# Gates of one branch moved from the merge stage into the RWKV stage's fillers, in a hybrid encoder layer on one Trainium2 core

## Chip, core and metric

The kernel runs on one core of one Trainium2 chip. The metric is the device time of one execution in microseconds (us). Lower is better.

## The reference

One encoder layer on 256 tokens of width 2048, all float32. Cut to what matters here:

```python
h = rms_norm(x, norm_mix_g)
a_cols, b_cols, c_cols, gate_cols = split(h @ w_in)
y_a = spatial_gating(a_cols)          # branch a
y_b = hyena_mixer(b_cols)             # branch b
y_c = rwkv7_mixer(c_cols)             # branch c: WKV scan, 16 heads, two directions
gates = sigmoid(gate_cols).reshape(bsz, seq, 3, D_MODEL)
merged = (gates[:, :, 0] * (y_a @ w_branch_a)
        + gates[:, :, 1] * (y_b @ w_branch_b)
        + gates[:, :, 2] * (y_c @ w_branch_c))
x = x + merged @ w_out
x = x + (silu(h2 @ w_ffn_gate) * (h2 @ w_ffn_up)) @ w_ffn_down     # h2 = rms_norm(x)
return rms_norm(x, norm_final_g)
```

A gate depends on `h` alone, which is known from the start. `y_c @ w_branch_c` needs all of `y_c`, so it can only be done when RWKV is over.

## The kernel before

**Dense products.** Activations stand channel by token: a tile has 128 channels by 256 tokens. Each float32 operand is split into a rounded high part and the rest, so that one product of a 128x128 weight block with 128x256 activations needs three matmuls: high by high, high by low, low by high. This kernel calls that a **step** of `dense` (L243 to L245, three matmuls of 256 columns). `dense_wide` does the same with two matmuls (L263: one of 512 columns that holds both parts of the activation, and L264: one of 256), and leaves two halves in PSUM that must be added afterwards. Weights come in **pieces** of four blocks, 256 KB: one DMA on SP's queue (L225), one cast on ACT (`wh`, L226), one subtraction (`wl`, L230) on DVE or POOL, whose share of the pieces is `pool_share`. There are five buffers each for `w`, `wh` and `wl`.

**RWKV and its fillers.** `rwkv` works on 8 pairs of heads. Each pair goes through five threads (preparation, scores, inverse, chain of four chunks, norm) made of small matmuls with DVE, ACT and POOL work between them. `threads` goes round all live threads, one part of each per **turn**. In each turn it also issues `ROUND` steps of dense work from a queue. That queue holds the projections of the next head pairs (`front`, labels c0 to c7, 48 steps each) and the merges of branch b (`merge_part`, label m, 16 steps for the gate and 8 for the branch, for each of 16 output tiles `n`). `more` feeds the queue. Where a projection isn't finished when its head pair starts, `need` issues the rest at once, with no thread's work between. What is left in the queue when the threads are done goes out in `drain`. Turns are a matter of program order; each engine runs its own instructions in that order and waits on semaphores.

**Last merges.** `merge_last` then does branch c for each `n`: 16 steps of `dense_wide` for the gate, two additions' worth of work and a tanh, 8 steps of `dense_wide` for the branch, and the sum into `macc`, whose split `mw` is the input of `outproj`. The sigmoid is written as tanh, with its factor folded in. In both versions the last part of an output is a chain through three engines: DVE (L1336) to POOL (L1337) to ACT (L1338) to DVE (L1339).

After that come `outproj` and `ffn`, which the change leaves alone.

The functions that the change touches, and their callers:

Of the kernel before, what the change touches and what calls it, by code (L numbers as in the profile page):

```python
# [9 lines left out]
F32 = mybir.dt.float32  # L10
F32R = mybir.dt.float32r
I32 = mybir.dt.int32
AF = mybir.ActivationFunctionType
ALU = mybir.AluOpType
PSUM = bass.MemoryType.PSUM

P = 128
T = 256
D = 2048
KD = D // P  # L20
# [10 lines left out]
KPIECE = 4  # L31
AHEAD = 3
LEN = {"conv": 9, "filter_mlp": 6, "filter_block": 14}
ROUND = 4.0
GC = 256
RS_MAGIC = float(0x5F1FFFF9)
RS_A = 2.38924456
# [87 lines left out]
def halves(x):  # L125
    return x[:, :, 0, :], x[:, :, 1, :]
# [68 lines left out]
class Build:  # L195
# [192 lines left out]
    def rwkv(self, rp, ych, ycl, y):  # L388
        nc, tc = self.nc, self.tc
        t = self.t  # L390
# [14 lines left out]
        for i in range(3):  # L405
            ps = self.pst("dn")
# [29 lines left out]

        front_weights = lambda j: [t["wc"][3 + 3 * j + i] for i in (1, 2, 0)]
        res, sts = {}, {}
        merges = iter(range(KD))

        def more():

            for n in merges:
                self.feed("m", self.merge_part(rp, n, 1, y, self.macc[:, n, :], False), (t["wgt"][n, 1], t["wbr"][n, 1]))
                return

        def preps():
            for j in range(NJ):
                self.need(f"c{j}")
                yield from self.wkv_prep(R, j, fronts[j], res)  # L450
                if j + 2 < NJ:
                    yield from self.after("v", j - 1)
                    self.feed(f"c{j + 2}", front(j + 2), front_weights(j + 2))

        def scores():
            for j in range(NJ):
                yield from self.after("prep", j)
                yield from self.after("chain", j - 2)
                yield from self.wkv_scores(R, j, res[j], sts)

        def inverses():
            for j in range(NJ):
                yield from self.after("blocks", j)
                yield from self.wkv_inverse(R, j, sts[j])

        def chains():
            for j in range(NJ):
                yield from self.after("inverse", j)
                yield from self.wkv_chain(R, j, res[j], sts.pop(j))

        def norms():
            for j in range(NJ):
                yield from self.after("chain", j)
                yield from self.wkv_norm(R, j, res.pop(j), ych, ycl)
# [3 lines left out]
        self.need("c0")  # L478
        self.pool_share = 0.6
        self.threads([norms(), chains(), inverses(), scores(), preps()], more)  # L480
        while len(self.queue) < KD:
            k = len(self.queue)
            more()
            if len(self.queue) == k:
                break
        self.drain()

    def threads(self, live, more):

        active, credit, still = 1, 0.0, 0  # L490
        while live:
            steps = 0
            for g in list(live):
# [3 lines left out]
                elif step:  # L497
                    steps += 1
                    credit += ROUND / active
                    while credit >= 1:  # L500
# [805 lines left out]
    def merge_part(self, p, n, b, y, out, first):  # L1306
# [10 lines left out]
        else:  # L1317
            nc.vector.scalar_tensor_tensor(th, th, 1.0, ps[:, :T], ALU.add, ALU.mult)
            nc.gpsimd.tensor_tensor(out, out, th, ALU.add)

    def merge_last(self, mp, y, mw):
        nc = self.nc
        for n in range(KD):
            m = self.macc[:, n, :]
            ps = self.pst("dn")
            self.dense_wide(self.t["wgt"][n, 2], lambda k: self.hw[:, k, :, :], ps)
            th = mp.tile([P, T], F32, tag="th", name="th", bufs=2)
            nc.vector.tensor_copy(th, ps[:, T:])
            nc.vector.tensor_tensor(th, th, ps[:, :T], ALU.add)
            nc.scalar.activation(th, th, AF.Tanh, scale=0.5)  # L1330
            ps = self.pst("dn")
            self.dense_wide(self.t["wbr"][n, 2], lambda k: y["c"][:, k, :, :], ps)
            s = mp.tile([P, T], F32, tag="s", name="s", bufs=2)
            nc.scalar.copy(s, ps[:, T:])
            nc.vector.tensor_tensor(s, s, ps[:, :T], ALU.add)
            nc.vector.scalar_tensor_tensor(th, th, 1.0, s, ALU.add, ALU.mult)  # L1336
            nc.gpsimd.tensor_tensor(m, m, th, ALU.add)  # L1337
            nc.scalar.activation(mw[:, n, 0, :], m, AF.Copy, scale=0.5)  # L1338
            nc.vector.scalar_tensor_tensor(mw[:, n, 1, :], m, 0.5, mw[:, n, 0, :].bitcast(F32), ALU.mult, ALU.subtract)  # L1339
# [102 lines left out]
```

## Time and profile before

| | us |
|---|---|
| median of three runs | 2011.07 (2007.12 to 2012.86) |
| the profiled execution, device time | 2020.24 |
| its span, first to last instruction | 2018.2 |
| busy PE, DVE, ACT, POOL | 1920.9, 1397.8, 1017.0, 562.2 |
| RWKV's turns, first to last of its small matmuls | 518.7 (510.4 to 1029.1) |
| dense work left over after them | 10.1 (1029.1 to 1039.2) |
| `merge_last` | 135.7 (1039.2 to 1174.9) |

Times of stages are those of PE's instructions. PE is TensorE (PEld its weight loads, which overlap), DVE is VectorE, ACT ScalarE, POOL GpSimd, SP the engine whose queue starts the weight DMAs. PEclk is the clock that TensorE was granted, 1.00 being 2.4 GHz and 0.50 being 1.2 GHz. "Busy" is a share of time with an instruction under way and not a measure of speed.

### The profile page before, as it was taken

To read this page: it belongs to the slowest core of one execution; us is meant where nothing else is said; L and a number is where in the kernel's file an instruction comes from. 1 tells how busy PE (TensorE), PEld (TensorE's weight loads), DVE (VectorE), ACT (ScalarE), POOL (GpSimd) and SP (SyncE) were. 2 spreads that over 40 slices of the span, in tenths; PEclk is the share of its full clock that TensorE was granted. 3 is DMA by queue.
4 is the path that set the end of the run, shared out by engine and by line. 5 is a ranking of instruction groups with operands and counts; after the bars stand their busy time and mean duration, and the time that the engine had idled before them with its cause. 6 is when DMAs were issued, how large, how long until landed. Compare 5 with 4: busy or idle time off the path is not lost.

```text
span 2018.2 us, 39307 instructions
## 1 busy us (share of the span) xinstructions
PE 1920.9 (95%) x14468; PEld 1734.5 (86%) x14468; DVE 1397.8 (69%) x2588; ACT 1017.0 (50%) x1958; POOL 562.2 (28%) x587
## 2 busy tenths in 40 slices
PE   7999999999879888998899999999999999999997
PEld 5899999999868787888898888888888888888886
DVE  7977788774777767677657667766666666655555
ACT  5665555545433344343445555555555555545443
POOL 5323232235645554455431121111111111100001
PEclk8999999999889899898999999999999999999999
DMA  7454444436343332333345565555555555666664
GB/s 233 159 167 156 142 146 144 155 132 197 115 105 95 103 99 84 105 104 91 104 151 186 187 225 188 187 190 190 190 191 190 189 190 191 190 187 185 187 187 136
DMA packets 215784, 320.51 MB, mean 159 GB/s; under 512 B 62182, under 2 KB 65768, under 8 KB 215592
## 3 DMA queue, kind: packets, MB, share of 16 engines
q1 hardware_dynamic: 209264, 306.13, 48.0%
q0 software_dynamic: 1984, 6.21, 1.0%
q10 hardware_dynamic: 4344, 5.67, 0.9%
q8 instruction: 113, 1.85, 0.4%
q14 instruction: 79, 0.65, 0.1%
HBM read 314.00 MB, written 3.93 MB: 158 GB/s over the span
## 4 chain that ended last, share of the span: by engine, by line
PE 82%; DVE 11%; DMA 3%; issue 2%; ACT 1%; SPq 0%; POOL 0%; DVEq 0%; ACTq 0%; POOLq 0%
PE ps_dn L263 23%; PE ps_dn L264 12%; PE ps_dn L243 9%; PE ps_big L263 8%; PE ps_dn L244 8%; PE ps_dn L245 8%; PE ps_big L264 4%; DVE Y L710 2%; PE ps_big L650 1%; DVE wl L230 1%; DVE Yt L709 1%; DMA Z<-d 1%; PE ps_ch L819 1%; PE ps_big L981 0%; DMA N<-d 0%
## 5 line engine op out<-in xcount | busy, mean ns | idle before, releaser
L226 ACT CAST wh<-w 128x512 fp32r<-128x512 f32 x1148 | 705.1, 619 | 655.0 <-PE ps_dn L263 260.6
L230 DVE TENSOR_TENSOR wl<-w,wh 128x512 fp32r<-128x512 f32 x945 | 711.4, 758 | 381.6 <-ACT wh L226 377.8
L243 PE MATMUL ps_dn<-hw,wh 128*128 128x256 f32 x1328 | 402.5, 303 | 1.6 <-ACT th L1312 1.2
L245 PE MATMUL ps_dn<-hw,wl 128*128 128x256 f32 x1328 | 382.9, 288 | 1.9 <-DVE wl L230 1.9
L244 PE MATMUL ps_dn<-hw,wh 128*128 128x256 f32 x1328 | 381.9, 288 | 0.0
L230 POOL TENSOR_TENSOR wl<-w,wh 128x512 fp32r<-128x512 f32 x203 | 273.3, 1350 | 383.9 <-ACT wh L226 345.0
L243 PEld LDWEIGHTS ps_dn<-hw,wh 128*128 128x128 f32 x1328 | 259.5, 195 | 12.4 <-issue 4.0
L245 PEld LDWEIGHTS ps_dn<-hw,wl 128*128 128x128 f32 x1328 | 259.5, 195 | 3.2 <-DVE wl L230 2.1
L244 PEld LDWEIGHTS ps_dn<-hw,wh 128*128 128x128 f32 x1328 | 259.7, 196 | 1.4
L263 PE MATMUL ps_dn<-gw,wh 128*128 128x512 f32 x704 | 246.3, 391 | 0.0
L263 PE MATMUL ps_big<-gw,wh 128*128 128x512 f32 x704 | 246.0, 391 | 0.0
L263 PE MATMUL ps_dn<-hid,wh 128*128 128x512 f32 x660 | 233.2, 396 | 0.0
L264 PE MATMUL ps_dn<-hid,wl 128*128 128x256 f32 x704 | 198.4, 282 | 0.0
L264 PE MATMUL ps_dn<-gw,wl 128*128 128x256 f32 x704 | 197.3, 280 | 0.0
L264 PE MATMUL ps_big<-gw,wl 128*128 128x256 f32 x704 | 197.1, 280 | 0.0
L263 PEld LDWEIGHTS ps_dn<-gw,wh 128*128 128x128 f32 x704 | 131.7, 187 | 28.9
L263 PEld LDWEIGHTS ps_big<-gw,wh 128*128 128x128 f32 x704 | 131.6, 187 | 28.9
L263 PEld LDWEIGHTS ps_dn<-hid,wh 128*128 128x128 f32 x660 | 124.0, 188 | 30.1
L264 PEld LDWEIGHTS ps_dn<-gw,wl 128*128 128x128 f32 x704 | 133.1, 189 | 0.1
L264 PEld LDWEIGHTS ps_big<-gw,wl 128*128 128x128 f32 x704 | 133.1, 189 | 0.0
L264 PEld LDWEIGHTS ps_dn<-hid,wl 128*128 128x128 f32 x704 | 132.2, 188 | 0.0
L1371 POOL TENSOR_TENSOR acc<-acc,sq 128x256 f32<-128x256 f32 x28 | 20.9, 745 | 292.3 <-ACT sq L1369 284.4
(395 smaller groups left out, 3369.0 us busy)
## 6 DMA issues: line engine op xcount, KB each, us to landing
w<-in_wgu_dram SPq DMA_DIRECT2D x352, 256.0 KB, 3.3
w<-in_wgt_dram SPq DMA_DIRECT2D x192, 256.0 KB, 3.1
w<-in_wdn_dram SPq DMA_DIRECT2D x176, 256.0 KB, 2.8
w<-in_wc_dram SPq DMA_DIRECT2D x108, 256.0 KB, 3.2
w<-in_wb_dram SPq DMA_DIRECT2D x96, 256.0 KB, 3.2
w<-in_wbr_dram SPq DMA_DIRECT2D x96, 256.0 KB, 2.7
w<-in_wo_dram SPq DMA_DIRECT2D x64, 256.0 KB, 3.4
w<-in_wav_dram SPq DMA_DIRECT2D x32, 256.0 KB, 3.7
```

The lines of the kernel that those rows point to most:

```text
L226: nc.scalar.copy(wh[:, :m], w[:, :m])
L230: e.tensor_tensor(wl[:, :m], w[:, :m], wh[:, :m].bitcast(F32), ALU.subtract)
L243: mm(ps, wh[:, i, :], xh[:, k, :], start=(k == 0), stop=False)
L244: mm(ps, wh[:, i, :], xl[:, k, :], start=False, stop=False)
L245: mm(ps, wl[:, i, :], xh[:, k, :], start=False, stop=(k == nk - 1))
L263: mm(ps, wh[:, i, :], xk.rearrange("p a t -> p (a t)"), start=(k == 0), stop=False)
L264: mm(ps[:, :T], wl[:, i, :], xk[:, 0, :], start=False, stop=(k == nk - 1))
L650: nc.tensor.matmul(ph[h][:, c * P:(c + 1) * P], bk[rows, d, c // 2, (c % 2) * P:(c % 2) * P + P], ar[rows, d, c, 1 - c % 2::1 + c % 2, :], ...
L709: V.tensor_tensor(z, N[:, k, k + 1:].unsqueeze(1).broadcast_to([P, w, n]), Y[:, :w, k:k + 1].broadcast_to([P, w, n]), mult)
L710: V.tensor_tensor(Y[:, :w, k + 1:], Y[:, :w, k + 1:], z, add)
L819: nc.tensor.matmul(pv[:, :P], ar[:, d, c, 0:2, :], R["sb"][i - 1][:, d, :], start=False, stop=(d == 1))
L1371: self.nc.gpsimd.tensor_tensor(acc, acc, s, ALU.add)
```

## The change

A new generator, `gate`, computes the gate of branch c for one output tile with 16 steps of `dense`, takes the tanh and stores the 128 KB result in a DRAM tensor, `gates`, by a DMA from POOL's queue. `more` now feeds merges of b and gates of c in turn, so the fillers of RWKV go from 768 steps to 1024. `ROUND` goes up by the same ratio, from 4 to 16/3. `merge_last` loads a gate by a DMA from POOL's queue, and does the branch with 8 steps of `dense` in place of 24 of `dense_wide`; the additions of PSUM halves and the tanh are gone from it.

```diff
-ROUND = 4.0
+ROUND = 16 / 3
...
-        merges = iter(range(KD))
+        self.gates = self.dp.tile([KD, P, T], F32, name="gates")
+        merges = iter([(n, b) for n in range(KD) for b in (1, 2)])
...
-            for n in merges:
-                self.feed("m", self.merge_part(rp, n, 1, y, self.macc[:, n, :], False), (t["wgt"][n, 1], t["wbr"][n, 1]))
+            for n, b in merges:
+                if b == 1:
+                    self.feed("m", self.merge_part(rp, n, 1, y, self.macc[:, n, :], False), (t["wgt"][n, 1], t["wbr"][n, 1]))
+                else:
+                    self.feed("g", self.gate(rp, n), (t["wgt"][n, 2],))
...
+    def gate(self, p, n):
+
+        ps = self.pst("dn")
+        yield from self.dense(self.t["wgt"][n, 2], self.hh, self.hl, ps[:, :T])
+        th = p.tile([P, T], F32, tag="th", name="th", bufs=1)
+        self.nc.scalar.activation(th, ps[:, :T], AF.Tanh, scale=0.5)
+        self.nc.gpsimd.dma_start(self.gates[n], th)
+
     def merge_last(self, mp, y, mw):
...
+            th = mp.tile([P, T], F32, tag="th", name="th", bufs=3)
+            nc.gpsimd.dma_start(th, self.gates[n])
             ps = self.pst("dn")
-            self.dense_wide(self.t["wgt"][n, 2], lambda k: self.hw[:, k, :, :], ps)
-            th = mp.tile([P, T], F32, tag="th", name="th", bufs=2)
-            nc.vector.tensor_copy(th, ps[:, T:])
-            nc.vector.tensor_tensor(th, th, ps[:, :T], ALU.add)
-            nc.scalar.activation(th, th, AF.Tanh, scale=0.5)
-            ps = self.pst("dn")
-            self.dense_wide(self.t["wbr"][n, 2], lambda k: y["c"][:, k, :, :], ps)
-            s = mp.tile([P, T], F32, tag="s", name="s", bufs=2)
-            nc.scalar.copy(s, ps[:, T:])
-            nc.vector.tensor_tensor(s, s, ps[:, :T], ALU.add)
-            nc.vector.scalar_tensor_tensor(th, th, 1.0, s, ALU.add, ALU.mult)
+            self.dense_all(self.t["wbr"][n, 2], *halves(y["c"]), ps[:, :T])
+            nc.vector.scalar_tensor_tensor(th, th, 1.0, ps[:, :T], ALU.add, ALU.mult)
```

Steps of `dense` in the order of PE's instructions, counted in the two built programs (the 1576 rows of small matmuls are the same in both):

| | before | after |
|---|---|---|
| between the first and the last small matmul of RWKV | 692 | 829 |
| of these issued at once by `need` | 77 | 9 |
| after the last small matmul, ahead of `merge_last` | 27 | 146 |
| in `merge_last` | 384 (wide) | 128 |

Lines from L440 on stand 4 or 5 lower in the changed kernel. On SP's queue, the last weight DMAs of RWKV before (`in_wgt_dram` holds gate weights, `in_wbr_dram` branch weights; the rows with d, N, Y and Z are RWKV's own):

```order
L225 DMA w<-in_wgt_dram 128x512 x3
L225 DMA w<-in_wbr_dram 128x512 x2
L225 DMA w<-in_wgt_dram 128x512
L716 DMA d_6479<-Y 32x8x16 x4
L225 DMA w<-in_wgt_dram 128x512 x2
L722 DMA Z<-d_6479 128x8x32
L225 DMA w<-in_wgt_dram 128x512
L225 DMA w<-in_wbr_dram 128x512 x2
L225 DMA w<-in_wgt_dram 128x512 x4
L225 DMA w<-in_wbr_dram 128x512 x2
L225 DMA w<-in_wgt_dram 128x512 x4
```

The same place after the change, down to the DMAs of `merge_last` (x32) and `outproj`:

```order
L225 DMA w<-in_wgt_dram 128x512 x6
L720 DMA d_6479<-Y 32x8x16 x4
L225 DMA w<-in_wbr_dram 128x512 x2
L726 DMA Z<-d_6479 128x8x32
L225 DMA w<-in_wgt_dram 128x512 x8
L225 DMA w<-in_wbr_dram 128x512 x2
L225 DMA w<-in_wgt_dram 128x512 x8
L225 DMA w<-in_wbr_dram 128x512 x2
...
L225 DMA w<-in_wgt_dram 128x512 x4
L225 DMA w<-in_wbr_dram 128x512 x32
L225 DMA w<-in_wo_dram 128x512 x64
```

Between two branch weights there are now eight pieces of gate weights (four for b, four for c), and more of them stand behind RWKV's last own DMA, Z.

On DVE in `merge_last` before, one output (L1328 and L1329 add up the gate's halves, L1335 the branch's; L1336 multiplies, L1339 splits the sum into `mw`):

```order
L1328 COPY th<-ps_dn 128x256
L1329 TENSOR_TENSOR th<-th,ps_dn 128x256
L230 TENSOR_TENSOR wl<-w,wh 128x512 x3
L1335 TENSOR_TENSOR s<-s,ps_dn 128x256
L1336 SCALAR_TENSOR_TENSOR th<-th,s 128x256
L230 TENSOR_TENSOR wl<-w,wh 128x512
L1339 SCALAR_TENSOR_TENSOR mw<-macc,mw 128x256
L230 TENSOR_TENSOR wl<-w,wh 128x512 x2
```

After the change, the start of `merge_last` and its first regular output (L1341 multiplies, L1344 splits):

```order
L230 TENSOR_TENSOR wl<-w,wh 128x512 x8
L1341 SCALAR_TENSOR_TENSOR th<-th,ps_dn 128x256 x2
L230 TENSOR_TENSOR wl<-w,wh 128x512
L1344 SCALAR_TENSOR_TENSOR mw<-macc,mw 128x256 x2
L230 TENSOR_TENSOR wl<-w,wh 128x512
L1341 SCALAR_TENSOR_TENSOR th<-th,ps_dn 128x256
L230 TENSOR_TENSOR wl<-w,wh 128x512
L1344 SCALAR_TENSOR_TENSOR mw<-macc,mw 128x256
L230 TENSOR_TENSOR wl<-w,wh 128x512
L1341 SCALAR_TENSOR_TENSOR th<-th,ps_dn 128x256
```

An output now has two weight pieces on DVE in place of six, one on each side of its split L1344. The pieces between L1341 of output n and L1341 of output n+1 belong to output n+3, so PE has two outputs' weights ahead.

On POOL at the end of the fillers and the start of `merge_last` after the change (L1331 stores a gate, L1338 loads one; before, POOL had there the `wl` pieces, L1319 and then sixteen L1337 in a row):

```order
L230 TENSOR_TENSOR wl<-w,wh 128x512 x4
L1331 DMA gates<-th 128x256
L230 TENSOR_TENSOR wl<-w,wh 128x512 x4
L1323 TENSOR_TENSOR macc<-macc,th 128x256
L1331 DMA gates<-th 128x256
L1338 DMA th<-gates 128x256 x3
L1342 TENSOR_TENSOR macc<-macc,th 128x256
L1338 DMA th<-gates 128x256
L1342 TENSOR_TENSOR macc<-macc,th 128x256
```

The gate stores stand among POOL's weight pieces, and the loads of the first three outputs stand behind the store of the last gate.

## Rows read from the trace of the kernel before

**Rows 1.** The profile's page: engines, and the granted clock in slices of 50.5 us.
```profile
PE 1920.9 (95%) x14468; PEld 1734.5 (86%) x14468; DVE 1397.8 (69%) x2588; ACT 1017.0 (50%) x1958; POOL 562.2 (28%) x587
...
PEclk8999999999889899898999999999999999999999
```

**Rows 2.** Busy time by stage: RWKV's turns, left-over fillers, merge_last.
```profile
core 0: us, PE busy (x) PEld busy (x) DVE busy (x) ACT busy (x) POOL busy (x), PEclk, DMA share, GB/s
510.40:1029.10 518.70, 456.66 (x5150) 415.55 (x5149) 363.47 (x866) 206.78 (x440) 262.81 (x276) 0.91 0.34 100
1029.10:1039.20 10.10, 9.99 (x83) 9.76 (x81) 8.92 (x16) 4.23 (x9) 4.48 (x4) 1.00 0.42 131
1039.20:1174.90 135.70, 135.69 (x768) 117.63 (x769) 95.35 (x176) 73.85 (x143) 18.21 (x16) 1.00 0.57 188
```

**Rows 3.** Waits of PE in RWKV's turns: total us, times, longest us.
```profile
PE ps_ch L819 <- DVE sb L853: 14.9, 9, 3.2
PE ps_inv L841 <- DVE UV L835: 11.6, 10, 3.7
...
PE ps_dn L245 <- DVE wl L230: 1.9, 1, 1.9
...
PE ps_big L650 <- DVE sc L653: 0.2, 1, 0.2
```

**Rows 4.** Stretches of 10 us in RWKV, columns as in Rows 2.
```profile
520.00:530.00 10.00, 4.25 (x25) 3.67 (x25) 9.90 (x14) 1.53 (x3) 6.35 (x8) 0.72 0.36 119
530.00:540.00 10.00, 8.72 (x58) 8.24 (x58) 6.10 (x8) 2.23 (x4) 4.25 (x6) 0.77 0.26 87
700.00:710.00 10.00, 10.00 (x72) 8.97 (x71) 5.57 (x11) 2.27 (x5) 3.23 (x3) 0.50 0.16 54
840.00:850.00 10.00, 10.00 (x86) 10.00 (x85) 3.77 (x7) 5.58 (x11) 7.26 (x6) 1.00 0.69 182
850.00:860.00 10.00, 6.13 (x59) 5.03 (x57) 9.22 (x35) 2.46 (x6) 1.80 (x2) 0.95 0.33 109
```

**Rows 5.** The chain that ended last in RWKV's turns, by line.
```profile
by line: PE ps_dn L243 12.1%; PE ps_dn L244 10.0%; PE ps_dn L245 9.9%; DVE Y L710 6.0%; PE ps_big L650 5.4%; DVE Yt L709 4.1%; DMA Z<-d 4.0%; issue 3.2%; PE ps_ch L819 2.3%; DMA N<-d 1.9%; DVE wl L230 1.8%; PE ps_inv L828 1.6%; PE ps_inv L8
```

**Rows 6.** PE in order of time: the first matmuls of two successive steps of `dense`.
```profile
1030.29 0.28 PE L243 MATMUL ps_dn<-hw,wh 128*128 128x256 f32 x1
...
1030.65 0.28 PE L243 MATMUL ps_dn<-hw,wh 128*128 128x256 f32 x1
```

**Rows 7.** DVE, then POOL, then ACT in merge_last, in order of time.
```profile
1099.44 0.69 DVE L230 TENSOR_TENSOR wl<-w,wh 128x512 fp32r<-128x512 f32 x1 [0.71 <-ACT wh L226]
1100.05 0.41 DVE L1335 TENSOR_TENSOR s<-s,ps_dn 128x256 f32<-128x256 f32 x1
1100.50 0.43 DVE L1336 SCALAR_TENSOR_TENSOR th<-th,s 128x256 f32<-128x256 f32 x1
...
1102.63 0.43 DVE L1339 SCALAR_TENSOR_TENSOR mw<-macc,mw 128x256 fp32r<-128x256 f32 x1 [1.08 <-ACT mw L1338]
1103.14 1.29 DVE L230 TENSOR_TENSOR wl<-w,wh 128x512 fp32r<-128x512 f32 x2
...
1101.00 1.15 POOL L1337 TENSOR_TENSOR macc<-macc,th 128x256 f32<-128x256 f32 x1 [7.33 <-DVE th L1336]
...
1102.18 0.42 ACT L1338 ACTIVATE mw<-macc 128x256 fp32r<-128x256 f32 x1 [1.35 <-POOL macc L1337]
```

**Rows 8.** Weight subtractions in RWKV's turns: busy us, mean ns, idle before.
```profile
L230 DVE TENSOR_TENSOR wl<-w,wh 128x512 fp32r<-128x512 f32 x35 | 26.7, 764 | 16.8 <-ACT wh L226 16.7
L230 POOL TENSOR_TENSOR wl<-w,wh 128x512 fp32r<-128x512 f32 x140 | 183.9, 1317 | 148.7 <-ACT wh L226 130.0 <-PE ps_inv L841 6.4 <-PE ps_dn L245 4.6
```

**Rows 9.** The DMAs of 128 KB from POOL's queue in RWKV's turns: issue ns, landing us.
```profile
L544 POOL DMA_DIRECT2D wa<-in_w2a_dram x7: 746/746/753, 527.8 to 872.5; - x7
...
DMA to landing us min/median/max: 2.5/2.8/4.0
```

**Rows 10.** The costliest wait of POOL in RWKV's turns: total us, times, longest us.
```profile
POOL wl L230 <- ACT wh L226: 130.0, 71, 8.0
```

More of the change, by code (lines that the diff above doesn't have):

```diff
@@ L480, in rwkv @@
         self.threads([norms(), chains(), inverses(), scores(), preps()], more)
-        while len(self.queue) < KD:
+        while len(self.queue) < 2 * KD:
             k = len(self.queue)
```

## The prediction

> **What bounds the kernel now.** The page of the profile comes first: PE is busy 1920.9 of 2018.2 us, and its clock is below full in the first slice and in a band of ten [rows 1]. Cutting the span into stages shows whose band that is: in RWKV's turns PE works 456.66 of 518.70 us at a mean clock of 0.91, while in the left-over fillers and in `merge_last` it works throughout at 1.00 [rows 2]. So time can be had in two ways: from PE's 62 us of idleness and its low clock in RWKV, or by giving PE less to do. The waits of PE say what the idleness is: 15 rows, the first and the last few of which are shown, 46 waits with 61.4 us in all, nearly all of them for DVE's part of the head pairs; only one, of 1.9 us, is for a weight piece [rows 3]. Stretches of 10 us show how it lies: DVE is full (9.90, 9.22) where PE is not (4.25, 6.13), and elsewhere PE is full and DVE is not [rows 4]. So RWKV alternates between a DVE bound and a PE bound. A dense step is free in the first kind of stretch and costs its whole time in the second.
>
> **What a step costs.** Two successive steps of `dense` start 0.36 us apart at full clock [rows 6]. `dense_wide` took 135.7 us for 384 steps [rows 2], 0.353 us each. The change therefore saves PE no work: 768 x 0.36 + 384 x 0.353 = 412.0 us before, 1152 x 0.36 = 414.7 us after. Everything depends on where the moved steps land.
>
> **Where they land.** By the count of steps, 137 of the 256 new ones get in among RWKV's turns, and 119 come after its last small matmul, where no wait of RWKV is left to fill. The second part is plain PE work, since the same work ran there gapless [rows 2]: 119 x 0.36 = **+42.8 us**.
>
> **RWKV's turns.** 137 steps more are +49.3 us of PE. Each turn gets 1.33 steps more, 0.48 us. Beside that, `need` issues 9 steps in one go in place of 77. Such a burst is PE's alone: from 840 to 850 PE is full with dense work while DVE does 3.77 us, and right after it DVE is full and PE has 3.87 us idle [rows 4]. Those 68 steps now go into turns, too, so that 205 steps (73.8 us) are in places where some can be hidden. How much is hidden isn't in the trace; three readings bound it:
> - If each of the 46 waits takes in only its own turn's 0.48 us, or all of it where it is shorter, 21 us vanish.
> - If the waits fill up wholly, 61 us do.
> - By the chain that ended last, the dense lines hold 12.1 + 10.0 + 9.9 = 32% of 518.7 us, 166 us [rows 5], while 692 steps at 0.36 are 249 us. A third of the dense time is off the path, so a third of 73.8 us, 25 us, would be. It is a little more, since some of the 166 us ran at the low clock.
>
> I take 30 us: near the chain's reading, which looks at the path itself, and a little above it because the bursts were wholly on it. The extra weight pieces are 34; with two fifths to DVE at 0.764 us that is 10.5 us of DVE [rows 8], which costs where DVE is full. DVE is busy for 363 of 518.7 us [rows 2], and full for less than half of the time, so I take 4 us between 0 and 10.5. POOL's three fifths, 20 x 1.317, and some 12 gate stores at 0.75 (the seven DMAs of the same size took 746 to 753 ns [rows 9]) are 36 us, beside 263 of 518.7 us [rows 2, 8]; POOL stands waiting for casts 130 us in that stage [rows 10], and I put them at nothing. If that cover is gone, rival D is the price. Together **+49.3 - 30 + 4 = +23 us**.
>
> **The last merges.** 128 steps at 0.36 are 46.1 us. But now each output leaves DVE less to do between two links of the chain that ends it. In the order on DVE, the multiply of output n+1 (L1341) stands behind a weight piece, that behind the split of output n (L1344), and the split waits for POOL's addition and ACT's copy of it. The same chain in the trace: the multiply starts at 1100.50, POOL at 1101.00, ACT at 1102.18, the split at 1102.63, the next weight piece at 1103.14; from a piece to the operation after it are 0.61 us (1099.44 to 1100.05) [rows 7]. So a round of DVE takes 2.64 + 0.61 = 3.25 us, where PE needs 8 x 0.36 = 2.88. Before, PE spent 8.5 us on an output and this was hidden. PE has two outputs' weights and two PSUM buffers ahead, so it isn't stopped in each round, but over the last 13 rounds it must fall in with DVE: 13 x 0.37 is 4.8 us, less about one output of slack (0.9 us) at the end, +4 us. The loads of the gates hide: issue 0.75 and landing 2.5 to 4.0 us [rows 9] against three buffers, 8.6 us of PE; the first ones wait for the last store, and are due only when PE wants its third PSUM buffer, 5.8 us in. POOL's 1.15 + 0.75 us per output fit into 3.25. The stage takes 50 us: **-85.7 us**. `outproj` and what follows stay as they are.
>
> **The sum.** +42.8 + 23 - 85.7 = -20 us. Against the profiled execution that is 2020.24 to 2000; it lies 9.2 us above the median of the runs shown, to which I apply the same difference: 2011.1 - 20 = **1991 us**.
>
> **Rivals.**
> - *A, as forecast,* -20 us, 1991; within the readings of what is hidden, 1975 to 2004. Chance 0.50.
> - *B, the clock comes back.* A mean of 0.91 [rows 2] means that about 18% of 518.7 us, 93 us, were at the lower level, 1.2 GHz, which cost up to 47 us. In 520 to 530 PE worked less than half of the time and the clock was 0.72; from 700 to 710 it worked all the time at 0.50 [rows 4]. Denser fillers leave PE less idle before; if half of the loss returns, the sum is -20 - 23 = -43 us, 1968. For it: every low stretch is in the stage with the waits. Against it: the DVE-bound stretches stay, and 0.48 us a turn doesn't fill 5.7 us in 10. I priced the clock at nothing in the sum. Chance 0.20. The Trainium skill, "TensorE: Matmul & The Clock Gate", section "Part 1: The HAM clock gate", says that the lower clock is the default and that sustained activity lifts it; by that rule this rival is the natural outcome, and the trace agrees so far as that idle and half clock come together.
> - *C, little is hidden.* 21 us hidden and DVE's 10.5 us in full: +42.8 + 49.3 - 21 + 10.5 - 85.7 = -4 us, 2007. For it: many waits sit at single links of the chain (46 waits, mean 1.3 us), and a later PE also delays what DVE waits for. Chance 0.13.
> - *D, the single buffer of the fillers' tanh; slower.* In `rwkv` the tile `th` has one buffer, and now the tanh of a merge, an instruction on ACT with the casts behind it, waits until the gate store before it has landed. The next tanh is 16 steps on, 5.8 us in the left-over fillers. A store that POOL issues at once takes 0.75 + 2.5 to 4.0 us [rows 9], which fits. Should POOL be 4 us behind its queue, half of its longest wait of 8.0 us [rows 10], ACT stands 4 + 0.75 + 4.0 - 5.8 = 3 us, and PE runs out of casts behind it. At 15 gates that is +44 us, total +24, 2035; it decides the sign from 1.3 us a gate. Against it: in the turns 16 steps are three turns, some 10 us, and only the last gates fall into the left-over part. Chance 0.10. The Trainium skill, "SBUF - State Buffer", section "Who interferes with whom", holds that a DMA issued from POOL can't write its descriptors while DVE holds the shared port pair, and gives 620 ns alone against 3100 ns beside a DVE copy; an estimate by that page is 2.35 us more at 32 DMAs, 75 us of POOL, which would bring this rival about. The seven issues at 746 to 753 ns beside a busy DVE don't show it [rows 9].
> - *E, the merge chain stops PE in each round.* If PE's second weight piece of an output is only ready after the split, PE's last 10 matmuls follow it in series: 2.64 + 0.69 + 10 x 0.12 + 0.25 = 4.8 us a round, 76 us for the stage, total +6 us, 2017. The order speaks against it, which has two outputs ahead. Chance 0.07.
>
> **How the numbers follow.** The forecast is A, 1991. Differences of under 0.3%, 6 us, are about what a measurement of this kernel can't tell from no change. A and B are faster, but for a twentieth of A that lies near the border; of C a third is faster and half the same; D is slower; E is on the border of the same and slower. That gives faster 0.72, same 0.14, slower 0.14. The range takes in B and E and half of what lies beyond them: 1960 to 2016; A alone would be 1975 to 2004.
>
> **What would show it.** Right: RWKV's turns take about 23 us more (542), the left-over fillers some 53 us (10.1 + 42.8) with PE full at 1.00, `merge_last` about 50 us with short PE gaps that end on PSUM of the output before last; PE's waits for DVE in the turns add up to some 30 us in place of 61. Wrong: turns that grow by 45 us and more (nothing hidden); a clock above 0.95 there with turns that hardly grow (B); waits of ACT's tanh for a store's DMA, or PE waiting for `wh` in the left-over fillers (D); a `merge_last` of over 60 us (E).

## The result and the profile after

The changed kernel is **slower**, by about 1%: 2034.77 us (median of four, 2031.53 to 2036.82) against 2011.93 us of the kernel before on the same chip (2007.12 to 2012.86), a ratio of 1.0106 with a 95% interval of 1.0078 to 1.0134. The forecast was 1991 us, 20 us faster. The profiled execution took 2036.82 us, its span 2035.0, 16.8 us more than the span before. The medians lie 22.8 us apart because the profiled execution of the kernel before was 8.3 us above its median, and that of the changed kernel 2.1.

The page of the changed kernel, engines and granted clock, answers to [rows 1]:

```profile
PE 1918.0 (94%) x14852; PEld 1751.7 (86%) x14852; DVE 1362.2 (67%) x2489; ACT 1008.8 (50%) x1942; POOL 645.1 (32%) x670
...
PEclk9999999999888899889999999999999999999999
```

The busy time by stage of the changed kernel, the same three stages as in [rows 2]:

```profile
510.40:1089.20 578.80, 499.89 (x5563) 462.46 (x5561) 382.53 (x871) 229.56 (x483) 302.60 (x314) 0.91 0.37 108
1089.20:1141.70 52.50, 52.50 (x439) 52.47 (x439) 17.42 (x26) 24.71 (x45) 38.45 (x34) 1.00 0.58 188
1141.70:1191.10 49.40, 48.27 (x388) 46.61 (x386) 31.63 (x61) 22.65 (x46) 24.27 (x32) 1.00 0.66 211
```

Two of the three stages came out as forecast: the left-over fillers take 42.4 us more (forecast 42.8), `merge_last` 86.3 us less (forecast 85.7). RWKV's turns take 60.1 us more, not the forecast 23. The three add up to +16.2 us, which is the difference of the spans but for 0.6 us. Within the turns, PE's busy time grew by 43.2 us (456.66 to 499.89), and its idle time, which the forecast saw shrink, by 16.9 us (62.0 to 78.9).

The waits of PE in the turns of the changed kernel (total us, times, longest us), where [rows 3] had 46 waits with 61.4 us; these are the first five and the two for weight pieces of 36 with 78.3 us:

```profile
PE ps_inv L734 <- DVE Z L729: 12.9, 5, 4.9
PE ps_inv L832 <- DVE T L825: 12.5, 9, 3.6
PE ps_ch L823 <- DVE sb L857: 10.9, 5, 3.6
PE ps_ch L823 <- DVE sb L859: 9.6, 2, 5.1
PE ps_ch L813 <- DVE UV L801: 8.2, 3, 5.0
...
PE ps_dn L245 <- POOL wl L230: 2.6, 1, 2.6
...
PE ps_dn L245 <- DVE wl L230: 1.4, 1, 1.4
```

There are fewer waits and they are longer; PE still waits for DVE's links of the head pairs. DVE in turn waits longer for PE. Its waits with `UV` for `ps_inv` were 11 with 10.3 us before (the longest 1.5); in the same view of the changed kernel they are

```profile
DVE UV L839 <- PE ps_inv L832: 19.5, 10, 3.9
```

The chain that ended last in the turns, by line, beside [rows 5]:

```profile
by line: PE ps_dn L243 12.0%; PE ps_dn L245 9.9%; PE ps_dn L244 9.6%; DVE Y L714 7.0%; DVE Yt L713 6.0%; PE ps_big L654 4.0%; issue 3.3%; DMA Z<-d 3.0%; DVE bk L614 2.1%; DVE wl L230 1.8%; PE ps_big L865 1.6%; DVE sb L857 1.6%; DMA N<-d 1.5
```

The dense lines hold 31.5% of 578.8 us, 182 us, 16 more than before. Y and Yt, two short operations on DVE whose work the change doesn't touch, hold 13.0%, 75 us, against 10.1% of 518.7 us, 52 us: 23 more. That was the surprise to follow. The groups of DVE and POOL in the turns of the changed kernel (busy us, mean ns, idle before); the two of L230 answer to [rows 8], and L714 and L713 had means of 394 and 286 ns before:

```profile
L230 POOL TENSOR_TENSOR wl<-w,wh 128x512 fp32r<-128x512 f32 x168 | 220.8, 1318 | 183.0 <-ACT wh L226 173.3 <-PE ps_dn L245 4.4 <-PE ps_inv L845 3.9
...
L714 DVE TENSOR_TENSOR Y<-Y,Yt 128x30 f32<-128x30 f32 (+10 forms) x120 | 52.0, 434 | 2.5
L713 DVE TENSOR_TENSOR Yt<-N,Y 128x30 f32<-128x30 f32 (+10 forms) x120 | 43.7, 364 | 5.8 <-DMA N<-d 3.3
...
L230 DVE TENSOR_TENSOR wl<-w,wh 128x512 fp32r<-128x512 f32 x41 | 32.7, 797 | 20.0 <-ACT wh L226 19.4 <-PE ps_inv L845 0.5
```

Of the 34 new weight pieces in the turns, 28 went to POOL (140 to 168) and 6 to DVE (35 to 41). The share of 0.6 sends four of five to POOL, not three of five: the fractions of `pieces * 0.6` (L228) that should equal 0.6 mostly fall just below it in floating point. [rows 8] show this already, 140 to 35.

What POOL's pieces do to DVE stands in the order of time. POOL, then DVE, from 566 us of the changed kernel:

```profile
566.48 0.75 POOL L548 DMA_DIRECT2D wa<-in_w2a_dram  x1 [0.29 <-POOL bk L615]
567.24 4.93 POOL L230 TENSOR_TENSOR wl<-w,wh 128x512 fp32r<-128x512 f32 x4
...
566.45 0.17 DVE L713 TENSOR_TENSOR Yt<-N,Y 128x14 f32<-128x14 f32 x1
566.66 5.55 DVE L714 TENSOR_TENSOR Y<-Y,Yt 128x14 f32<-128x14 f32 x1
572.25 0.19 DVE L713 TENSOR_TENSOR Yt<-N,Y 128x26 f32<-128x26 f32 x1
```

One addition on DVE (L714 adds two SBUF tiles) of 14 columns, 0.17 us by its neighbours, took 5.55 us. It began while POOL issued a DMA, ended at 572.21, just after the four weight pieces behind that DMA (572.17), and it lies on the chain. It is the longest by far, but the rule is plain: of the 240 instructions of these two lines, 56 took more than 0.4 us, and each of the 56 ended 0.03 to 0.06 us after a POOL instruction beside it did. Split the 120 instructions of each line by whether POOL worked during more than 5% of them. Alone, 80 of L714 took 0.180 us in the mean, none over 0.2; beside POOL, 40 took 0.938. At L713 it is 81 at 0.181 and 39 at 0.745. The excess is 40 x 0.758 + 39 x 0.564 = 52 us in these two lines; the same split of before (L709: 36 at 0.530; L710: 43 at 0.774) gives 38 us. The Trainium skill, "SBUF — State Buffer", section "Who interferes with whom", states that a DVE instruction with two inputs in SBUF contends with a GpSimd instruction that reads SBUF; the trace agrees, and its 5.55 us show the size.

### The profile page after: what moved, and what is told of

Same layout as the page of the kernel before. It is cut to its first block, busy times and chain, and to the rows that moved or that the text cites. A ratio compares the mean times of both kernels' runs of the same rounds, so it can differ in the third digit from the quotient of the medians.

```text
span 2035.0 us, 40092 instructions
## 1 busy us (share of the span) xinstructions
PE 1918.0 (94%) x14852; PEld 1751.7 (86%) x14852; DVE 1362.2 (67%) x2489; ACT 1008.8 (50%) x1942; POOL 645.1 (32%) x670
## 4 chain that ended last, share of the span: by engine, by line
PE 79%; DVE 14%; DMA 3%; issue 2%; ACT 1%; SPq 1%; POOL 0%; DVEq 0%; ACTq 0%; POOLq 0%
PE ps_dn L263 18%; PE ps_dn L243 10%; PE ps_dn L245 10%; PE ps_dn L264 10%; PE ps_dn L244 10%; PE ps_big L263 8%; PE ps_big L264 4%; DVE Y L714 2%; DVE Yt L713 2%; DVE wl L230 2%; PE ps_big L654 1%; DMA Z<-d 1%; DVE bk L614 1%; DMA w<-in_wav_dram 1%; PE ps_big L985 0%
## 5 line engine op out<-in xcount | busy, mean ns | idle before, releaser
L230 DVE TENSOR_TENSOR wl<-w,wh 128x512 fp32r<-128x512 f32 x894 | 678.4, 763 | 394.5 <-ACT wh L226 390.2
L243 PE MATMUL ps_dn<-hw,wh 128*128 128x256 f32 x1584 | 482.0, 304 | 3.7 <-DVE rk L386 2.5
L230 POOL TENSOR_TENSOR wl<-w,wh 128x512 fp32r<-128x512 f32 x254 | 339.7, 1342 | 427.4 <-ACT wh L226 399.2
L245 PE MATMUL ps_dn<-hw,wl 128*128 128x256 f32 x1584 | 458.9, 290 | 4.0 <-POOL wl L230 2.6
L244 PE MATMUL ps_dn<-hw,wh 128*128 128x256 f32 x1584 | 457.0, 289 | 0.0
L243 PEld LDWEIGHTS ps_dn<-hw,wh 128*128 128x128 f32 x1584 | 312.0, 197 | 16.0 <-issue 5.9
L245 PEld LDWEIGHTS ps_dn<-hw,wl 128*128 128x128 f32 x1584 | 312.1, 197 | 5.4 <-POOL wl L230 2.8
L244 PEld LDWEIGHTS ps_dn<-hw,wh 128*128 128x128 f32 x1584 | 312.5, 197 | 1.3
```

What stands on the lines that cost most here:

```text
L230: e.tensor_tensor(wl[:, :m], w[:, :m], wh[:, :m].bitcast(F32), ALU.subtract)
L243: mm(ps, wh[:, i, :], xh[:, k, :], start=(k == 0), stop=False)
L244: mm(ps, wh[:, i, :], xl[:, k, :], start=False, stop=False)
L245: mm(ps, wl[:, i, :], xh[:, k, :], start=False, stop=(k == nk - 1))
```

## The experiments

Two theories were set against each other. **F**: the moved steps are paid in full, since PE's instructions stand in one order and a step ahead of a small matmul makes DVE's next input late by as much as it fills. **K**: the extra weight pieces cost, because POOL's subtractions hold up DVE. All times below are medians; stages are from the profiled execution. "Idle" is the length of the turns less PE's busy time there. e2, e3 and e4 were executed once each.

**e1_round4**: the changed kernel with the old density of fillers.

```diff
-ROUND = 16 / 3
+ROUND = 4.0
```

> The changed kernel with ROUND back at 4.0: gates of c stay among the fillers, but the turns get no more steps than before (668 steps between RWKV's small matmuls in place of 829, and 307 in place of 146 left over behind them). Theory F (PE runs in order, so each step of a turn stands in front of the head pairs' small matmuls and is paid in full): RWKV's turns fall from 579 us to about 512, the left-over fillers take 307 x 0.36 = 110 us in place of 52.5, merge_last stays at 49; about 2025 us. Theory K (the weight work of the denser fillers on POOL and DVE slows DVE's own operations): the same here. If both are wrong and the gates' own stores and tanhs cost the time, RWKV's turns stay above 540 us.

Measured 2024.38 us, ratio 1.0060 (1.0036 to 1.0084). The turns hold 668 steps in place of 829 and take 508.6 us in place of 578.8, 0.44 us a step; the left-over fillers grow to 111.6 us, 0.37 a step. So a step is dearer in the turns than behind them. Idle is 69.2 us: fewer fillers don't leave more of it than the 78.9 of the denser version. (POOL's pieces change along with the steps here, 136 in place of 168.)

**e2_nosub**: no subtraction for the pieces of c's gates (their low part is left out).

```diff
+        if light:
+            return v(wh), v(wh)
         wl = self.wp.tile([P, 128 * KPIECE], F32R, tag="wl", name="wl", bufs=5)
```

> The changed kernel, but the pieces of branch c's gate weights get no subtraction: the third matmul of their steps takes the cast weights again, so that the low part of these weights is left out. PE's and ACT's work is the same, POOL and DVE lose 64 subtractions. Theory F: RWKV's turns stay at 570 us or more. Theory K: they fall to 545 us or less, and DVE's two-operand operations in the inverse (L713, 364 ns in the mean) go back to about 290 ns.

Measured 2018.49 us; turns 562.6, 16.2 us less. The turns as a row of the windows, and the weight pieces that are left (L233 of this run is L230 of the others):

```profile
508.20:1070.80 562.60, 492.72 (x5561) 455.74 (x5560) 360.35 (x861) 229.09 (x483) 249.06 (x274) 0.93 0.38 111
L233 POOL TENSOR_TENSOR wl<-w,wh 128x512 fp32r<-128x512 f32 x128 | 166.7, 1306 | 126.3 <-ACT wh L225 100.0 <-issue 17.9 <-PE ps_inv L847 2.1
L233 DVE TENSOR_TENSOR wl<-w,wh 128x512 fp32r<-128x512 f32 x31 | 23.5, 758 | 21.0 <-ACT wh L225 19.0 <-DMA N<-d 2.0
```

The length lies between the two expectations; the mean of Yt fell from 364 to 300 ns, as K has it. So K is real, and isn't all. This run also tests F by itself. It has 829 steps in the turns, but 128 and 31 subtractions on POOL and DVE, fewer than the 140 and 35 of the kernel before, and Y and Yt are as short as there (389 and 300 ns against 394 and 286). Even so idle is 69.9 us, 7.9 more than the 62.0 before: the denser fillers hid nothing, and that isn't because their own subtractions filled the room again.

**e3_onemm**: all the steps of c's gates issue one matmul of three (the other two products are left out), so the pieces stay and PE's work goes.

```diff
+                if one:
+                    mm(ps, wl[:, i, :], xh[:, k, :], start=(k == 0), stop=(k == nk - 1))
+                    yield
+                    continue
```

> The changed kernel, but a step of branch c's gates issues only one of its three matmuls (the other two products are left out). DMAs, casts and subtractions are the same; PE loses 384 matmuls of 0.12 us in RWKV's turns, 46 us at full clock, and 128 in the left-over fillers, 15 us. Theory F: RWKV's turns fall by 45 us or more, to about 530, since PE's steps are on the path. Theory K: they stay at 560 us or more.

Measured 1993.16 us; turns 539.3. 384 matmuls of 0.12 us, 46 us, were taken out of the turns; 39.5 come back, 36.5 of them as PE's busy time; idle stays at 75.9. Most of F, then: what is put in is paid, and what is taken out doesn't turn into waits.

**e4_pool45** and **e7_after45**: fewer pieces on POOL in the turns; nothing else. **e5_before45** does the same to the kernel before, as the control.

```diff
-        self.pool_share = 0.6
+        self.pool_share = 0.45
```

> The changed kernel with pool_share 0.45 in place of 0.6 in RWKV, so that POOL gets some 94 weight pieces in its turns in place of 125 (before the change some 105) and DVE 31 more. Theory F: RWKV's turns stay within 8 us of 579. Theory K with POOL as the culprit: they fall by 10 to 20 us, as DVE's operations run less often beside POOL's. Theory K with DVE's own load as the culprit: they grow by 10 us or more.

Measured 2011.02 us; turns 551.0. The two groups of the weight pieces:

```profile
L230 POOL TENSOR_TENSOR wl<-w,wh 128x512 fp32r<-128x512 f32 x94 | 124.4, 1324 | 185.7 <-ACT wh L226 179.0 <-PE ps_ch L813 2.7 <-PE ps_inv L845 2.3
L230 DVE TENSOR_TENSOR wl<-w,wh 128x512 fp32r<-128x512 f32 x114 | 84.5, 741 | 58.2 <-ACT wh L226 57.6
```

74 pieces left POOL. DVE took them on, 52 us of work, and yet is busy only 14 us more (396.8 against 382.5): its other work shrank from 349.8 to 312.3 us, 0.5 us for each piece that POOL no longer does. K's mechanism is shown, for the price of a POOL piece is paid on DVE. (That PE waits for the slower pieces of POOL isn't it: at share 0.6 those waits are 2.6 us in all.)

> The kernel before the change with pool_share 0.45 in place of 0.6 in RWKV: the control of the run before. Theory K (each subtraction on POOL lengthens DVE's operations beside it, whatever the density of the fillers): POOL's pieces in the turns go from 140 to about 79, and RWKV's turns fall from 519 us by about 20, to some 499; about 1992 us. If POOL's subtractions only hurt with the denser fillers, the turns stay within 5 us of 519 and the time at about 2010.

Measured 1999.60 us, ratio 0.9921 (0.9894 to 0.9948); turns 493.6, 25 us less. The kernel before gains nearly as much, so this is no repair of the change.

**e6_after30**, share 0.3 (in fact 40% of the pieces, 84 of 209):

> The changed kernel with pool_share 0.3. Theory K, POOL the culprit without a limit: RWKV's turns fall from 551 us at 0.45 by another 10 us or more. If DVE's own subtractions take over, they stay or grow.

Measured 1996.66 us, ratio 0.9916 (0.9886 to 0.9946); turns 538.3, another 10 to 13 us less than at 0.45, as by K.

> The changed kernel with pool_share 0.45 again, timed: about 2011 us, the same as before the change, since RWKV's turns of 551 us in place of 578 give back what the change cost.

Measured 2010.00 us, ratio 0.9972 (0.9952 to 0.9993); turns 548.6.

**e8_round4_45** and **e9_round267**: share 0.45 and `ROUND` 4.0 and 8/3.

> The changed kernel with ROUND 4.0 and pool_share 0.45 together. If the two causes add up (POOL's subtractions 27 us in the turns, the denser turns more than the left-over fillers give), RWKV's turns take about 490 us, the left-over fillers 111 and merge_last 49: about 2004 us. Theory F alone: as ROUND 4.0 alone, 2017 to 2025 us.

Measured 2004.70 us, ratio 0.9952 (0.9936 to 0.9969).

> The changed kernel with ROUND 8/3 and pool_share 0.45: 534 steps between RWKV's small matmuls, 441 behind them. Theory F (a step in the turns is paid in full at any density): against ROUND 4.0 with 0.45 the turns lose 134 x 0.41 = 55 us, to about 428, and the left-over fillers gain 134 x 0.36 = 48: about 1998 us. If steps were free at low density because DVE binds there, the turns stay above 455 us and the time goes above 2020.

Measured 2012.55 us, ratio 1.0004 (0.9983 to 1.0025). The turns of these two and of e7, with 534, 668 and 829 steps, as rows of the windows (columns as in [rows 2]). e9:

```profile
508.30:953.00 444.70, 395.20 (x4674) 351.69 (x4674) 347.69 (x896) 181.00 (x394) 156.56 (x192) 0.95 0.35 94
```

e8:

```profile
510.20:993.50 483.30, 433.47 (x5076) 392.03 (x5076) 373.30 (x918) 203.63 (x435) 183.73 (x214) 0.96 0.39 106
```

e7:

```profile
509.00:1057.60 548.60, 487.67 (x5561) 448.76 (x5560) 397.67 (x944) 229.70 (x483) 210.85 (x240) 0.95 0.40 114
```

A step costs (483.3 - 444.7) / 134 = 0.29 us between the first two and 65.3 / 161 = 0.41 between the last two, so "in full at any density" is not exact. But idle is 49.5, 49.8 and 60.9 us: denser fillers never lower it, and the cheaper steps between e9 and e8 are cheaper in PE's busy time, which stays unexplained. POOL has 61, 76 and 94 pieces in these turns; since idle stayed the same from 61 to 76, some hiding at the low density, set off by POOL's cost, can't be excluded.

**e12_dense_alone**: the kernel before with `ROUND` 16/3 and share 0.45, density without the gates.

> The kernel before with ROUND 16/3 and pool_share 0.45: the denser turns alone, without the gates. The same fillers go out earlier and none is left at the end. Theory F: the sum of work is the same and nothing more is hidden, so the time is that of the kernel before at 0.45, 2000 us, within 6. If density itself is harmful, it is 2010 us or more; if denser turns hide something, 1990 or less.

Measured 2024.42 us, ratio 1.0066 (1.0046 to 1.0086), 25 us above e5. Not the clean test it was meant to be: all 719 steps of the queue are gone before the turns end, and the last turns run without fillers. Stretches of 20 us of it:

```profile
980.00:1000.00 20.00, 19.75 (x218) 17.55 (x214) 14.21 (x45) 10.21 (x22) 5.15 (x6) 1.00 0.47 126
1000.00:1020.00 20.00, 15.37 (x294) 12.41 (x293) 10.62 (x35) 4.33 (x10) 0.00 (x0) 0.91 0.31 77
1020.00:1040.00 20.00, 15.34 (x124) 12.68 (x126) 10.10 (x31) 4.03 (x11) 0.72 (x1) 0.58 0.00 1
1040.00:1060.00 20.00, 12.52 (x55) 9.34 (x54) 9.11 (x21) 5.37 (x12) 1.46 (x2) 0.56 0.08 26
1060.00:1080.00 20.00, 20.00 (x117) 17.62 (x117) 14.50 (x27) 10.86 (x21) 2.25 (x2) 1.00 0.60 185
```

Without fillers PE idles and the granted clock falls to 0.56. The run says nothing of density itself.

**The share taken further, on both kernels**: 0.25 (e10 and e11, again as e13 and e14), 0.1 (e15, e16) and 0 (e17, e18).

> The kernel before with pool_share 0.25, so that POOL gets 43 weight pieces in the turns in place of 140 (79 at 0.45). Theory K without a limit: the turns fall from 494 us at 0.45 by another 10 to 15, to about 481; about 1987 us. If DVE's own load takes over, they stay at 494 or grow.

> The changed kernel with pool_share 0.25 (51 pieces in place of 168). The same question at the higher density: by K alone the turns fall from 538 us at 0.3 to about 526. By F it stays behind the kernel before at the same share by 8 to 15 us, since 137 more steps cost 55 us in the turns and only 43 us less than the last merges give back is left over.

> The kernel before with pool_share 0.25 again, on one chip with the changed kernel at the same share: 1993 us.

> The changed kernel with pool_share 0.25 again, to stand beside the one before at the same share. If the change is worth nothing without POOL's subtractions: within 4 us of 1993. If the fillers hide a part as forecast, 12 us or more below it; if F holds as at 0.45, 10 us above it.

> The kernel before with pool_share 0.1: some 17 weight pieces on POOL in the turns in place of 43. If POOL's subtractions are the harm down to the last, the turns fall below 490 us; if DVE's load has taken over, they grow above 500 us and the time passes 1998.

> The changed kernel with pool_share 0.1, some 21 pieces on POOL. DVE then has some 186 subtractions of 0.73 us in the turns, 136 us. If DVE's load has taken over, the turns grow above 538 us; if not, they stay at 528 or fall.

> The kernel before with no weight subtraction on POOL in RWKV's turns. If POOL's subtractions harm down to the last, about 1970 us; if the last ones relieved DVE, 1977 or more.

> The changed kernel with no weight subtraction on POOL in RWKV's turns: the same question at the higher density. If the change is worth nothing by itself, within 4 us of the kernel before at the same share; if the denser fillers hide better the less POOL does, 5 us or more below it.

Measured, beside the runs above (us; idle of PE in the turns and pieces on POOL there):

| share | kernel | median | ratio (95%) | turns | idle | on POOL |
|---|---|---|---|---|---|---|
| 0.6 | before | 2011.9 | | 518.7 | 62.0 | 140 |
| 0.6 | after | 2034.8 | 1.0106 (1.0078 to 1.0134) | 578.8 | 78.9 | 168 |
| 0.45 | before (e5) | 1999.6 | 0.9921 (0.9894 to 0.9948) | 493.6 | 52.4 | 79 |
| 0.45 | after (e7) | 2010.0 | 0.9972 (0.9952 to 0.9993) | 548.6 | 60.9 | 94 |
| 0.25 | before (e10) | 1993.4 | 0.9914 (0.9894 to 0.9935) | 495.2 | 46.9 | 44 |
| 0.25 | after (e11) | 1992.7 | 0.9900 (0.9870 to 0.9931) | 528.4 | 51.4 | 53 |
| 0.25 | before (e13) | 1985.4 | 0.9874 (0.9851 to 0.9896) | 494.9 | 46.8 | 44 |
| 0.25 | after (e14) | 1989.3 | 0.9888 (0.9862 to 0.9915) | 529.8 | 48.1 | 53 |
| 0.1 | before (e15) | 1976.5 | 0.9825 (0.9795 to 0.9855) | 478.4 | 36.3 | 17 |
| 0.1 | after (e16) | 1973.3 | 0.9814 (0.9780 to 0.9848) | 511.8 | 36.1 | 21 |
| 0 | before (e17) | 1965.8 | 0.9767 (0.9731 to 0.9802) | 468.9 | 29.5 | 0 |
| 0 | after (e18) | 1972.0 | 0.9798 (0.9765 to 0.9832) | 515.3 | 30.0 | 0 |

Three things follow. Idle falls with the pieces on POOL in both kernels, to half and less. The change never lowers it by more than 0.2 us: at share 0 it is 29.5 and 30.0 us, and what the change adds to it shrinks as POOL's pieces do (16.9 us at share 0.6, 8.5 at 0.45, 4.5 and 1.3 at 0.25, -0.2 at 0.1). That isn't the price of the added pieces alone: from 0.6 to 0 idle falls by 0.23 us for each piece in the kernel before (32.5 us for 140) and by 0.29 in the changed one (48.9 for 168), so that 28 more pieces come to some 6 to 8 us. And at shares of 0.25 and less no gain of the change can be told from noise. Against the kernel before on the same chip its median is 0.7 us lower and 3.9 higher at 0.25, 3.2 lower at 0.1 and 6.2 higher at 0; in the last case only one of the six times of e17 is above any of e18, so that it is rather a loss there. (The same program differed by 8 us between two chips, e10 and e13.)

One expectation was missed: from 0.45 to 0.25 the turns of the kernel before didn't fall (493.6 to 495.2). Idle fell by 5.5 us there, but PE's busy time rose by 7; at 0.1 they fell to 478.4. At share 0, the turns of e17 as a row of the windows:

```profile
508.30:977.20 468.90, 439.43 (x5149) 399.28 (x5149) 380.65 (x1005) 206.26 (x440) 85.75 (x136) 0.97 0.38 111
```

the weight pieces of e17 in the turns, all of them on DVE:

```profile
L230 DVE TENSOR_TENSOR wl<-w,wh 128x512 fp32r<-128x512 f32 x174 | 124.6, 718 | 38.4 <-ACT wh L226 36.0 <-DMA Z<-d 0.7 <-DMA w<-in_wc_dram 0.7
```

and the turns of e18, with Yt and Y in them:

```profile
507.10:1022.40 515.30, 485.34 (x5559) 447.78 (x5559) 400.98 (x1037) 229.41 (x483) 94.89 (x146) 0.96 0.41 121
...
L713 DVE TENSOR_TENSOR Yt<-N,Y 128x30 f32<-128x30 f32 (+10 forms) x120 | 27.8, 232 | 1.6
...
L714 DVE TENSOR_TENSOR Y<-Y,Yt 128x30 f32<-128x30 f32 (+10 forms) x120 | 25.8, 215 | 1.6
```

DVE does every subtraction, and in e17 it is busy only 17 us more than at 0.6 (380.65 against 363.47): its other work fell from 336.8 to 256.1 us, 0.58 us for each of 140 pieces. Yt and Y, at 364 and 434 ns with 168 pieces on POOL, are at 232 and 215 ns with none. Of the 49.8 us that e17's turns are shorter than those before, 32.5 are idle and 17.2 are PE's busy time, at a granted clock of 0.97 in place of 0.91. Between e17 and e18 the change adds 46.4 us to the turns and takes 43.2 off the two stages behind (145.6 to 102.4): +3.2 us, the difference of the two spans.

**The version that beats both** is e17, the kernel before with no weight subtraction on POOL in RWKV: 1965.8 us, 2.3% under it.

## Why the prediction was wrong

- **The left-over fillers** (+42.8) were right, +42.4, gapless at 1.00 as forecast.
- **`merge_last`** (-85.7) was right, -86.3, and for its reason. In the order of time DVE's split comes every 3.22 us (forecast 3.25), with the wait for POOL and ACT that the prediction described, and PE stops for 0.11 to 0.12 us at each of the last seven outputs:

```profile
1157.25 0.42 DVE L1344 SCALAR_TENSOR_TENSOR mw<-macc,mw 128x256 fp32r<-128x256 f32 x1 [1.08 <-ACT mw L1343]
1157.76 0.69 DVE L230 TENSOR_TENSOR wl<-w,wh 128x512 fp32r<-128x512 f32 x1
1158.37 0.41 DVE L1341 SCALAR_TENSOR_TENSOR th<-th,ps_dn 128x256 f32<-128x256 f32 x1
1158.70 0.68 DVE L230 TENSOR_TENSOR wl<-w,wh 128x512 fp32r<-128x512 f32 x1
1160.47 0.43 DVE L1344 SCALAR_TENSOR_TENSOR mw<-macc,mw 128x256 fp32r<-128x256 f32 x1 [1.09 <-ACT mw L1343]
```

- **RWKV's turns, "I take 30 us" hidden: the step that failed.** Two of the three readings that bounded it (21 and 61 us) took PE's waits as room that more steps fill. The runs show that they aren't: idle went up in place of down, it rose by 7.9 us even with fewer subtractions than before (e2), and with POOL's pieces out of the way it stayed the same to 0.5 us. The likely reason is PE's order: a step stands ahead of a later small matmul, so that DVE's next link starts later as well, and the wait comes after it. The third reading (25 us) failed, too: that the share of the dense lines on the chain is under their busy time was no measure of what a further step costs. Of 137 steps at 0.36, 49.3 us, PE's busy time shows 43.2; no other hiding is seen.
- **The extra pieces, "I put them at nothing" for POOL: the second step that failed.** The count was off (28 on POOL, not 20) and the price was sought on the wrong engine: POOL had room, but each of its pieces holds up DVE. The trace of before showed it (0.18 us alone, 0.53 and 0.77 beside POOL), in two lines that [rows 5] list on the chain. e2 gives the price: 50 subtractions fewer in the turns (40 on POOL, 10 on DVE) gave back 16.2 us, 9.0 of idle and 7.2 of PE's busy time. In proportion the 34 extra ones cost some 11 us, an estimate, in place of the 4 forecast.
- Together: with 11 us for the pieces, 49 of the 60.1 us are left for the 137 steps, which is their full 49.3: +49 and +11 in place of +49.3, -30 and +4, a miss of 37 us, the whole way from -20 to +17. The break-even follows from the terms that were right: the two stages behind give back 43.9 us for 137 steps, 0.32 each, so that the change could only win if a step cost less than that in the turns. It cost 0.44 with POOL's part and 0.34 without (46.4 / 137, share 0). The profiles at shares of 0.25 and 0.1 show 0.24 to 0.25, but those of e11 and e16 are of the fastest execution of each, 9.5 and 6.3 us under its median, and the medians show no such gain.
- **Rivals.** C had the mechanism ("a later PE also delays what DVE waits for"), but still let 21 us vanish, and gave 2007. B didn't come: the clock's mean stayed at 0.91, and idle didn't shrink; where idle did shrink, at share 0, the clock is 0.97 and 0.96. That idle and half clock come together holds by stage only: [rows 4] have a full PE at 0.50 and one of 6.13 us in 10 at 0.95. D's time, 2035, is the measured one, but by luck, for nothing that it rests on happened. (The 620 and 3100 ns that it takes from the Trainium skill, "SBUF — State Buffer", stand there in the section "A bandwidth-pool intuition that's wrong (but worth ruling out)".) E didn't come either. The rows of the gates' DMAs, with what idled before and who waited:

```profile
L1331 POOL DMA_DIRECT2D gates<-th x16: 557/580/601, 601.1 to 1143.1; - x16
...
  ACT th L1330: 11.8, 4
...
  DVE th L1341: 0.5, 1
...
DMA to landing us min/median/max: 2.0/3.3/4.3
```

Stores issue in 0.58 us beside a busy DVE; POOL idles for the tanh and not the other way round (the tanh, L1330, has no wait in the trace), and 0.5 us of waiting for a loaded gate is all.

**What stays open.** Why a step costs 0.29 to 0.41 us of the turns by density, and 33 us in all for 137 steps at shares of 0.25 and 0.1 but 46 at 0: the stage differs by some 10 us from one version to the next in PE's busy time at nearly equal clocks, and no run separated this. Nor is it shown why the 7.9 us of idle that the change adds in e2, without its own subtractions, are gone at share 0. That the later start of DVE's links is what keeps idle constant is argued from PE's order and the longer waits of DVE for PE (19.5 against 10.3 us at `UV`); no run held the links' times fixed.

## What to carry to other kernels

An idle engine in a chain of dependent work isn't by itself room for more of its work: here 137 steps of filler more took nothing off the idle time, most likely because filler that stands in order ahead of the chain's next link moves the link. Before pricing work on a second engine at nothing, split the instructions of the bounding engine by whether that second engine ran beside them; a mean that hides 0.18 and 0.94 us is a price. And test a suspected cost on the kernel before as well: here most of what looked like a repair of the change was a gain that had nothing to do with it.

## What the runs showed of the hardware

- A short operation on two SBUF tiles on DVE, 0.18 us alone, ends with the POOL instruction that it meets: all 56 of 240 that took over 0.4 us in the changed kernel ended 0.03 to 0.06 us after one, and all but one took 1.7 us at most. That one, an addition, was held for 5.55 us, through a DMA issue of POOL and four subtractions of 128x512 back to back. In the mean a POOL piece of 1.32 us lengthened DVE's other work by 0.5 to 0.58 us.
- DVE does such a piece in 0.71 to 0.80 us in the mean, so that giving POOL 140 of 175 relieved DVE of 97.9 us of subtractions (124.6 us at share 0, 26.7 at 0.6) and cost it 80.7 us of its other work.
- Where fillers ran out, the granted clock was 0.91, 0.58 and 0.56 in the next three stretches of 20 us, with PE busy for 15.4, 15.3 and 12.5 us of each, and 1.00 in the stretch after them, where PE was full.
